# An overflow expert's tokens 65 to 96 computed before the branch for the tokens past 96

## The chip, the cores and the metric

The kernel runs on one core of one Trainium2 chip. The metric is the device time of one execution in microseconds (us). TensorE (PE; PEld is its weight load) does the matmuls, VectorE (DVE) and ScalarE (ACT) the elementwise work, and the queue of SyncE (SP) issues the loads of the weights.

## The reference, cut to what matters

256 tokens pass through a layer of attention and convolution, then a mixture of 32 experts, then a second block. The part that the change touches is the mixture:

```python
logits = (xt @ router_w + router_b).astype(jnp.float32)
top_vals, top_idx = lax.top_k(logits, 4)
top_w = jax.nn.softmax(top_vals, axis=-1)
combine = jnp.einsum('tk,tke->et', top_w, jax.nn.one_hot(top_idx, 32))
...
u = xt @ w1 + b1                     # w1 of an expert: 1024 x 2048
glu = jnp.minimum(u[:, ::2], 7.0)
lin = jnp.clip(u[:, 1::2], -7.0, 7.0)
a = glu * jax.nn.sigmoid(1.702 * glu) * (lin + 1)
out = a @ w2 + b2                    # w2 of an expert: 1024 x 1024
acc = acc + gate_e[:, None] * out
```

Each expert's weights are 12 MB in float32. An expert needs to compute only the tokens that chose it. With the inputs of this case the router sends 65 tokens to expert 5, 81 to expert 16, and at most 56 to any other; none gets more than 96.

## The kernel before

The weights of the whole program stream through a ring of SBUF slots in a fixed order: `w1` of an expert (8 slots of 1 MB), its `w2` (4 slots), `w1` of the next expert, and so on. All loads are issued by SP's queue, in order (lines 169, 175 and 190, in `pump`). A load into a used slot waits until the last reader of that slot is done. `ring.release` is called for the `w1` slots behind `over()` and for the `w2` slots behind the second matmul.

The loop over the 32 experts (from line 1213) gathers an expert's first 64 tokens by a one-hot matmul, multiplies by `w1` (`w1_mm`, line 1076), applies the gated activation on DVE and ACT (`glu`, lines 1088 to 1092), multiplies by `w2` (`w2_mm`, lines 1100 to 1108, or `w2_mm32`, lines 1114 to 1121, with up to 32 tokens) and scatters the result into the accumulators Y (`scatter`, line 1135). Between `glu` and the scatter of the expert before stands `over()`: under a branch on the count (line 1237) the code for tokens past 64. There `wide` handles 64 tokens from 96 on, under its own branch (line 1171), and calls itself for 160 and 224; `narrow` handles tokens 65 to 96: one-hot on DVE (`pmc` line 1030, `S_x` line 1034), gather (line 1040), scatter matrix (lines 1055 to 1059), `w1_mm`, `glu`, `w2_mm32`, scatter with `GT_x`. Both read the expert's `w1` and `w2` slots again, and both use the buffers S_x, GT_x, M2 and misc0.

Two facts of the program's text matter below. Each matmul adds one to a counter of PE; where a branch skips a body, a block on the other side (the else block) waits for what precedes it on PE and then adds the body's whole number at once, so that the count behind the branch is the same either way. And a load into a slot waits for the count of the last instruction, in the order of the program, that reads the slot.

A prefetch hint for PE at the start of an expert (`over_hint`, line 1164) names the branch of line 1237 and, in a register, which way it will go; DVE and ACT have none.

## Time and profile before

| | us |
|---|---|
| time, median of 3 runs | 1654.56 (1653.56 to 1656.74) |
| the profiled execution, time | 1654.44 |
| the profiled execution, span of its instructions | 1652.6 |
| PE busy | 1440.6 (87%) |
| DVE busy | 577.4 (35%) |
| ACT busy | 408.5 (25%) |
| weights read, at what mean rate | 531.60 MB, 322 GB/s |

The span runs from the first to the last instruction; 1.8 us of the execution lie outside it. The experts run from about 203 to 1157 us. In a row of the page with 40 slices a slice is 41.3 us. In rows of work, `128x32` and the like are partitions by elements; `[5.65 <-DVE S_x L1034]` is the idle time of the engine just before, and what ended it. A name with q (PEldq, SPq) is the engine's sequencer: it branches, waits or issues.

### The profile page before, as it was taken

Reading aid. Unit: us, or ns where it says so; the run is one execution under the profiler, and the core shown is the slowest. Engines: PE = TensorE matmul, PEld = TensorE weight load, DVE = VectorE, ACT = ScalarE, POOL = GpSimd, SP = SyncE. Lnnn points to the kernel's source line nnn. Section 1 sums busy time; section 2 is a strip of 40 time slices with the busy share of each in tenths; the row PEclk is TensorE's granted clock in tenths of the full one; section 3 lists DMA queues with packets and bytes.
Section 4 is the critical chain, followed back from the end, with each engine's and each line's share of the span. In section 5 each row is a group of like instructions: output and inputs, shape, how many; then the busy total and the mean of one; then the engine's idle time right before and its main releaser. Section 6 shows DMA issues by size and latency. Waiting matters only on the chain. (4 is left out here: it accounts for less than half of the span.)

```text
span 1652.6 us, 22025 instructions
## 1 busy us (share of the span) xinstructions
PE 1440.6 (87%) x9176; PEld 874.2 (53%) x9176; DVE 577.4 (35%) x1028; ACT 408.5 (25%) x664; POOL 19.8 (1%) x23
## 2 busy tenths in 40 slices
PE   5999988888987787687988898776999999999998
PEld 2877733343322332333333332321867999899997
DVE  2466602112210211111111111111896556565655
ACT  3455301001100001001000110001536344463434
POOL 0000200000000000000000000000000001000000
PEclk9999998979989879888998999888999999999999
DMA  9767899988999999999999999999915535245420
GB/s 392 289 258 300 318 399 398 423 360 344 423 422 420 423 421 420 422 377 386 424 419 389 424 420 421 423 422 419 363 49 205 212 147 223 109 180 228 167 88 26
DMA packets 66825, 535.27 MB, mean 324 GB/s; under 512 B 6992, under 2 KB 7504, under 8 KB 17104
## 3 DMA queue, kind: packets, MB, share of 16 engines
q1 hardware_dynamic: 65744, 531.36, 78.3%
q8 instruction: 132, 2.16, 0.5%
q10 hardware_dynamic: 896, 1.31, 0.2%
q14 instruction: 53, 0.43, 0.1%
HBM read 531.60 MB, written 1.05 MB: 322 GB/s over the span
## 5 line engine op out<-in xcount | busy, mean ns | idle before, releaser
L1076 PE MATMUL U<-ra,M 128*32 128x512 f32 (+1 forms) x1248 | 205.2, 631 | 42.1 <-DMA ra<-in_w_dram 36.1
L378 PE MATMUL G<-hTh,whl 128*128 128x256 f32 x720 | 201.2, 279 | 1.0 <-DVE whl L361 1.0
L376 PE MATMUL G<-hTh,whl 128*128 128x256 f32 x720 | 201.2, 279 | 0.1
L377 PE MATMUL G<-hTl,whl 128*128 128x256 f32 x720 | 200.9, 279 | 0.0
L361 DVE TENSOR_TENSOR whl<-ra,whl 128x1024 fp32r<-128x1024 f32 x160 | 185.9, 1221 | 21.0 <-ACT whl L358 20.9
L358 ACT ACTIVATE whl<-ra 128x1024 fp32r<-128x1024 f32 x159 | 156.7, 1046 | 7.5 <-ACT whl L358 4.8
L1088 DVE TENSOR_SCALAR M<-U 128x256 f32<-128x256 f32 (+1 forms) x34 | 17.9, 527 | 363.4 <-PE U L1076 363.4
L1076 PEld LDWEIGHTS U<-ra,M 128*32 128x32 f32 (+1 forms) x1248 | 51.6, 122 | 170.7 <-issue 121.1
L378 PEld LDWEIGHTS G<-hTh,whl 128*128 128x128 f32 x720 | 135.5, 188 | 1.4 <-DVE whl L361 1.4
L376 PEld LDWEIGHTS G<-hTh,whl 128*128 128x128 f32 x720 | 135.5, 188 | 1.1 <-ACT whl L358 0.3
L377 PEld LDWEIGHTS G<-hTl,whl 128*128 128x128 f32 x720 | 135.5, 188 | 0.7
L1089 ACT ACTIVATE M<-M 128x256 f32<-128x256 f32 (+1 forms) x34 | 17.0, 499 | 429.0 <-DVE M L1088 429.0
L1126 DVE SCALAR_TENSOR_TENSOR M<-misc,gc,g2hc 128x512 f32<-128x512 f32 x32 | 24.0, 751 | 230.2 <-PE misc L1108 123.9
L1135 PE MATMUL Y<-OO,GT 64*128 64x512 f32 x256 | 44.5, 468 | 54.6 <-PEq L1237 52.8
L1076 PE MATMUL U<-rc,M 128*64 128x512 f32 (+1 forms) x400 | 74.8, 634 | 11.3 <-DMA rc<-in_w_dram 11.3
L1050 ACT ACTIVATE M<-misc 128x512 f32<-128x512 f32 x32 | 19.1, 597 | 262.7 <-PE misc L1049 262.7
L1076 PE MATMUL U<-wa,M 128*32 128x512 f32 (+1 forms) x416 | 76.8, 622 | 0.1
L1049 PEld LDWEIGHTS misc<-S,h 128*128 128x128 f32 x512 | 59.6, 192 | 25.6 <-issue 25.6
L1135 PEld LDWEIGHTS Y<-OO,GT 64*128 64x128 f32 x256 | 27.7, 211 | 84.3 <-issue 79.3
L376 PE MATMUL Y<-whl,gh 128*128 128x512 f32 x176 | 69.5, 395 | 0.0
L376 PE MATMUL Y<-hTh,whl 128*128 128x256 f32 x224 | 66.3, 296 | 3.7 <-ACT whl L358 3.0
L377 PE MATMUL Y<-whl,gh 128*128 128x512 f32 x176 | 69.4, 394 | 0.0
(408 smaller groups left out, 2061.7 us busy)
## 6 DMA issues: line engine op xcount, KB each, us to landing
ra<-in_w_dram SPq DMA_DIRECT2D x64, 2048.0 KB, 24.7
ra<-in_w_dram SPq DMA_DIRECT2D x94, 1024.0 KB, 19.3
wa<-in_w_dram SPq DMA_DIRECT2D x71, 1024.0 KB, 22.9
rc<-in_w_dram SPq DMA_DIRECT2D x21, 2048.0 KB, 25.3
rc<-in_w_dram SPq DMA_DIRECT2D x30, 1024.0 KB, 24.1
ra<-in_w_ada_dram SPq DMA_DIRECT2D x24, 1024.0 KB, 11.9
ra<-in_w_up_dram SPq DMA_DIRECT2D x21, 1024.0 KB, 6.0
ra<-in_w_down_dram SPq DMA_DIRECT2D x21, 1024.0 KB, 7.0
```

What stands on the lines that cost most here:

```text
L358: act.activation(self.t[j][:, 0, :], src, AF.Copy)
L361: dve.tensor_tensor(self.t[j][:, 1, :], self.w[:, 1024 * j:1024 * (j + 1)], self.t[j][:, 0, :].bitcast(F32), ALU.subtract)
L376: pe.matmul(ps, lh, rh, start=start, stop=False)
L377: pe.matmul(ps, lh, rl, start=False, stop=False)
L378: pe.matmul(ps, ll, rh, start=False, stop=stop)
L1049: pe.matmul(ps[:, k], h2[:, t, kk * P:(kk + 1) * P], Sp[:, :, t, 0:C], start=(t == 0), stop=(t == 1))
L1050: act.activation(xg[:, 4 * q:4 * q + 4], ps, AF.Copy)
L1076: pe.matmul(U[o:o + n, j // m, :], xg(k), w1s[k][:, 512 * j:512 * (j + 1)], start=(k == 0), stop=(k == KT - 1), tile_position=(0, o))
L1088: dve.tensor_scalar(g, uv[:, :, :, 0], 7.0, None, ALU.min)
L1089: act.activation(s_, g, AF.Sigmoid, scale=1.702)
L1126: dve.scalar_tensor_tensor(t32, o_ps, gc, g2hc, ALU.mult, ALU.mult)
L1135: pe.matmul(y[t][h], GT[hs, t * P:(t + 1) * P], o[hs, :], start=False, stop=stop and o is ol)
```

## The change

`over()` calls `narrow` first and `wide` behind it, so that the branch of line 1171 on the count past 96 stands behind the work on tokens 65 to 96. The outermost branch of `wide` gets a label in `over()`, and a hint for it on PE, DVE and ACT is placed first in the body of `over()`.

```diff
     def wide(base, cv, e, S_x, sel, w1s, w2s, oh, ol):
-        with tc.If(cv > base):
+        with tc.If(cv > base, label=f"rest{e}" if base == C + 32 else None):
...
         def over():
             with tc.If(cv_e > C, label=f"over{e}"):
+                tc.mark_branch_hint_location(f"rest{e}", hint=cv_e > C + 32, engines=[ET.PE, ET.DVE, ET.Activation])
+                narrow(e, S_x, sel, w1s, w2s, Oh[b], Ol[b])
                 wide(C + 32, cv_e, e, S_x, sel, w1s, w2s, Oh[b], Ol[b])
-                narrow(e, S_x, sel, w1s, w2s, Oh[b], Ol[b])
```

From here on line numbers are those of before up to 1237; behind it the new program's are one higher.

On PE, at the start of an overflow body (here expert 5's; rc, wa and ra are slots of the ring), before:

```order
L1237 COMPARE_AND_BRANCH
L1171 COMPARE_AND_BRANCH
L1040 MATMUL misc_1737<-S_x,h_1543 128x64 x16
L1055 MATMUL misc_1737<-comb,S_x 128x1 x2
L1057 MATMUL misc_1737<-cst,S_x 128x128 x2
L1076 MATMUL U<-rc_3990,M_1714 64x512 x4
```

and now:

```order
L1237 COMPARE_AND_BRANCH
L1238 REGISTER_ALU
L1744 BRANCH_PREFETCH_HINT
L1040 MATMUL misc_1737<-S_x,h_1543 128x32 x16
L1055 MATMUL misc_1737<-comb,S_x 128x1 x2
L1057 MATMUL misc_1737<-cst,S_x 128x128 x2
L1076 MATMUL U<-rc_4026,M_1714 32x512 x4
```

The 32-wide gather has moved up to the branch of line 1237, and the branch of line 1171 is gone from ahead of it.

On PE, at the end of expert 5's `narrow`, before:

```order
L1135 MATMUL Y_110<-OO,GT_x 128x512
L1135 MATMUL Y_109<-OO,GT_x 128x512
L1135 MATMUL Y_110<-OO,GT_x 128x512
L1237 UNCONDITIONAL_BRANCH x2
L1067 TENSOR_LOAD cnt
L1135 MATMUL Y_107<-OO,GT_1730 128x512
```

and now:

```order
L1135 MATMUL Y_110<-OO,GT_x 128x512
L1135 MATMUL Y_109<-OO,GT_x 128x512
L1135 MATMUL Y_110<-OO,GT_x 128x512
L1171 COMPARE_AND_BRANCH
L1040 MATMUL misc_1737<-S_x,h_1543 128x64 x16
L1055 MATMUL misc_1737<-comb,S_x 128x1 x2
L1057 MATMUL misc_1737<-cst,S_x 128x128 x2
L1076 MATMUL U<-rc_4026,M_1714 64x512 x4
```

Behind the scatter of `narrow` now stand the branch of line 1171 and the three bodies of `wide`, whose matmuls on the `w1` slots (the last row, for one slot) are the last in the program to read them. SP's loads stand in the same order as before.

## Rows read from the trace of the kernel before

**Rows 1.** The page, 40 slices of the span: share of the weight-load engines, rate

```profile
DMA  9767899988999999999999999999915535245420
GB/s 392 289 258 300 318 399 398 423 360 344 423 422 420 423 421 420 422 377 386 424 419 389 424 420 421 423 422 419 363 49 205 212 147 223 109 180 228 167 88 26
```

**Rows 2.** Stretches: length, busy time by engine, granted clock, DMA share, GB/s

```profile
364.00:374.00 10.00, 9.48 (x58) 4.24 (x61) 0.16 (x1) 0.77 (x2) 0.00 (x0) 0.63 0.36 132
402.00:410.00 8.00, 7.08 (x63) 2.30 (x56) 2.72 (x9) 0.42 (x1) 0.00 (x0) 1.00 0.20 51
706.00:708.00 2.00, 2.00 (x24) 0.60 (x20) 0.00 (x0) 0.00 (x0) 0.00 (x0) 1.00 0.82 311
729.00:733.00 4.00, 4.00 (x22) 1.36 (x20) 0.00 (x0) 0.00 (x0) 0.00 (x0) 1.00 0.84 324
740.00:748.00 8.00, 7.18 (x64) 2.36 (x57) 1.80 (x5) 0.42 (x1) 0.00 (x0) 1.00 0.30 107
895.00:901.00 6.00, 2.16 (x14) 1.42 (x13) 2.87 (x5) 0.63 (x1) 0.00 (x0) 0.95 0.52 191
```

**Rows 3.** Timeline of SP's queue: start, length, line, load, count

```profile
371.22 0.33 SPq L190 DMA_DIRECT2D wa<-in_w_dram  x1
...
407.71 0.33 SPq L190 DMA_DIRECT2D rb<-in_w_dram  x1
...
706.32 0.33 SPq L190 DMA_DIRECT2D wa<-in_w_dram  x1
...
745.79 2.02 SPq L190 DMA_DIRECT2D ra<-in_w_dram  x4
...
898.79 2.57 SPq L190 DMA_DIRECT2D ra<-in_w_dram  x4
```

**Rows 4.** Waits of SP's queue, 355 to 415 us: total, times, longest

```profile
SPq L190 <- PE U L1076: 26.5, 2, 26.0
...
SPq L190 <- PEq L1237: 11.5, 1, 11.5
```

**Rows 5.** Line 1171, by stretch around each overflow: count, shortest/median/longest ns, start

```profile
L1171 PEldq COMPARE_BRANCH  x1: 7517/7517/7517, 350.4 to 350.4; - x1
...
L1171 PEldq EVENT_SEMAPHORE  x1: 51/51/51, 358.0 to 358.0; - x1
...
L1171 PEldq COMPARE_BRANCH  x1: 7295/7295/7295, 686.0 to 686.0; - x1
```

**Rows 6.** Timeline of PE and DVE around the two overflow starts

```profile
350.92 1.94 PE L1076 MATMUL U<-ra,M 128*64 128x512 f32 x8
...
355.86 0.17 DVE L1030 TENSOR_SCALAR pmc<-posm 128x2 f32<-128x2 f32 x1
358.07 0.48 DVE L1034 TENSOR_SCALAR S_x<-cst,pmc 128x128 f32<-128x128 f32 x2 [2.04 <-PEq L1171]
...
358.51 7.01 PE L1040 MATMUL misc<-S_x,h 128*128 128x32 f32 x32 [5.65 <-DVE S_x L1034]
...
693.40 0.48 DVE L1034 TENSOR_SCALAR S_x<-cst,pmc 128x128 f32<-128x128 f32 x2 [1.84 <-PEq L1171]
```

**Rows 7.** Timeline of PE at the end of each `narrow`

```profile
386.43 0.96 PE L1135 MATMUL Y<-OO,GT_x 64*128 64x512 f32 x6 [0.23 <-DVE OO L1128]
...
723.05 1.65 PE L1135 MATMUL Y<-OO,GT_x 64*128 64x512 f32 x6 [0.23 <-DVE OO L1128]
```

**Rows 8.** Line 1237 and its hint on PE, whole span: count, shortest/median/longest ns

```profile
L1237 PEldq COMPARE_BRANCH  x34: 78/444/6930, 206.0 to 1145.1; - x34
...
L1743 PEldq BRANCH_PREFETCH_HINT  x32: 30/35/44, 202.7 to 1123.3; - x32
```

**Rows 9.** PE behind a skipped line 1237, by two experts; and last wait for weights

```profile
302.26 1.20 PE L1135 MATMUL Y<-OO,GT 64*128 64x512 f32 x8 [0.57 <-PEq L1237]
...
865.18 1.20 PE L1135 MATMUL Y<-OO,GT 64*128 64x512 f32 x8 [4.00 <-PEq L1237]
...
1143.25 1.94 PE L1076 MATMUL U<-rc,M 128*32 128x512 f32 x8 [3.28 <-DMA rc<-in_w_dram]
```

**Rows 10.** Stretches of PE at half clock (columns as in rows 2)

```profile
357.70:371.40 13.70, 12.37 (x58) 9.04 (x62) 0.64 (x3) 0.77 (x2) 0.00 (x0) 0.50 0.62 261
692.20:705.90 13.70, 11.54 (x54) 8.84 (x58) 0.64 (x3) 0.77 (x2) 0.00 (x0) 0.50 1.00 419
866.30:873.10 6.80, 6.05 (x22) 3.18 (x22) 0.16 (x1) 0.98 (x2) 0.00 (x0) 0.50 0.99 405
```

## Prediction

> **What bounds the kernel now.** The page's slices come first. From slice 10 on (413 us) the rate stands at 420 to 424 GB/s almost throughout the experts; the exceptions are slices 8 and 9 (330 to 413 us, 360 and 344), 17 and 18 (702 to 785 us, 377 and 386) and 21 (868 to 909 us, 389) [rows 1]. So the experts run at the speed of the weight loads, and what costs time there is a stretch in which no load is under way. The last expert still waits 3.28 us for its weights at 1143 us [rows 9], so a load that comes later ends the expert stage later by as much.

> Next, where the load engines starve [rows 2]. Behind expert 5's first matmuls: 364 to 374 us at a share of 0.36, and 402 to 410 us at 0.20. Behind expert 16's: 706 to 708 at 0.82, 729 to 733 at 0.84, 740 to 748 at 0.30. And 895 to 901 at 0.52. These are the slices with the low rate, and two of the three groups are the two experts that enter the overflow code.

> Then what ends each gap. SP's next loads start at 371.22 and 407.71, and at 706.32, 745.79 and 898.79 [rows 3]. The one at 371.22 had waited 26.0 us for a `w1` matmul of PE (L1076), the one at 407.71 had waited 11.5 us for the sequencer at L1237 [rows 4]. This contrast is the row to look at. At 407.71 the expert is an ordinary one: its `w1` matmuls were done, but the last reader of its slots in the program is the skipped overflow body, so the load waits for the else block of L1237, which adds the skipped count. At 371.22 `narrow` had been entered and was itself the last reader, so slots came free matmul by matmul, in the middle of its `w1`.

> Last, the branch that moves. On PE, the branch at L1171 takes 7.5 us at expert 5 and 7.3 at expert 16 [rows 5]: a jump over the unused code. DVE has `pmc` at 355.86 and then sits 2.04 us (1.84 at expert 16) until that branch lets it write S_x; PE sits 5.65 us in all [rows 6].

> **The change part by part.** The profile gives each term; all of them happen twice, at experts 5 and 16. Where a branch is not entered nothing is added to the instructions that run.

> *The front of the overflow.* The branch leaves the head, so S_x follows `pmc` at once: 2.04 us earlier at expert 5, 1.84 at expert 16 [rows 6], and all of `narrow` with it. The hint costs PE some 35 ns [rows 8], and its register instruction, as an estimate, the same; DVE and ACT run theirs while PE is late anyway, so I count nothing, and with that cover gone 0.1 us.

> *The clock.* Both gathers run at half the granted clock (0.50 for 13.7 us [rows 10]), behind 5.65 us of idle PE. The idle shrinks to some 3.6 us. [...] An idle of 4.00 us elsewhere was followed by 0.50 [rows 9, 10], which is the nearest row, so I take 0, with 5.4 as the other end.

> *The back of the overflow.* Behind `narrow`'s scatter PE meets L1171 and jumps. With an effective hint the price is that of a skipped L1237: 0.57 us of idle PE [rows 9]. Without, that branch took 7.5 [rows 5]; with the matmuls still in flight some 6 of these remain. Of the hinted branches of L1237 the shortest took 78 ns, the median 444 and the longest 6930 [rows 8]; most are short, and here the hint comes some 35 us ahead (350.4 [rows 5] to about 385), so I take 0.6. In the loads' account PE's 0.6 is hidden, since the loads wait for the else block and not for what PE does behind it.

> [...]

> *The release of the slots: the term that decides.* Now the three bodies of `wide` stand last in the program and read `w1`. So at experts 5 and 16 the refill no longer waits for `narrow`'s own `w1` matmuls but for the else block of L1171, behind `narrow`'s last matmul; this is the ordinary expert's case of 11.5 us [rows 4], with the whole of `narrow` in between. SP's queue is in order, so every later load is queued behind that one, and the loads issued before had all landed when the gap began.

> Expert 5: `narrow`'s last matmul ends at 386.43 + 0.96 = 387.39 [rows 7]; less 2.04 it is 385.35. The refill moves from 371.22 [rows 3] to there: **+14.1 us** of empty queue. Against it stands the second gap. From 385.4 the queue has the 8 slots of `w1` and soon the 4 of `w2`, 12 loads of 1.05 MB, 29.8 us at 422 GB/s, to about 416; the next expert frees its slots at 407.71 less about 1.4. So the gap of 402 to 410, 8 x 0.80 = **6.4 us**, goes. Net **+7.7**.

> Expert 16: the last matmul ends at 723.05 + 1.65 = 724.70 [rows 7], less 1.84 = 722.86; the refill moves there from 706.32: **+16.5**. Here the queue was just running out at 706 (0.82 in that stretch), so up to 1.5 us of it may still be covered. The gaps of 729 to 733 (4 x 0.16 = 0.6) and 740 to 748 (8 x 0.70 = 5.6) go, since the refill lasts 29.8 us to 753 and the next release comes at 745.79. Net **+10.3**.

> Slice 21: the gap of 895 to 901 (6 x 0.48 = **2.9**) arises since PE lags the loads. They are 10 us later against PE than before, so the release at 898.79 comes in time. **-2.9**.

> Do PE's own inputs suffer? Expert 6's `w1` is in SBUF when the queue runs dry, its `w2` is the first thing refilled, four loads or 10 us, done by 397 and needed behind 408. So PE does not wait within the gap, and the delay shows as later weights only.

> Sum against the profiled execution: 1654.44 + 7.7 + 10.3 - 2.9 = **1669.5 us**; it lies 0.1 under the median of the runs, so this is the predicted median too.

> **The rivals.**

> 1. *Faster: the release doesn't move.* If a slot of an overflow expert were still freed by `narrow`'s matmuls, or if the loads had enough other slots, only front and back would count: -2.04 - 1.84 + 2 x 0.6 = -2.7, about 1652, and 1642 with the clock's 5.4 twice. It decides on whether the first load behind the gap follows `narrow`'s `w1` or its end. Against it: the wait of 11.5 us at L1237 shows that a skipped last reader holds the slots. Such a time is within 0.2% (3.3 us, about what a measurement of this kernel can tell from no change) of the time before, or a little better. 5%.

> 2. *The hint at L1171 does not work.* The branch then ends some 6 us behind the last matmul, and the else block with it: +6 at each expert, 1675.5 for one, 1681.5 for both. For: the slowest branches of L1237 had a hint as well (6930 ns). 13%, mostly for one.

> 3. *The clock stays up.* Both `narrow` end up to 5.4 us earlier: 1669.5 - 10.8 = 1659 at the least, 1664 with one of the two. 12%.

> 4. *The gap at 895 us stays*, since PE comes to wait for the later weights and releases late again: 1672.4. 8%.

> **How the numbers follow.** The forecast as summed, within some 3 us for the tail of the queue at 706 us and the run-to-run scatter, has 62%. The range must reach rival 4, one clock of rival 3 and one failed hint: **1663 to 1677**, which leaves out both hints failing, both clocks staying, and rival 1. Slower by over 0.2%: 0.94; within: 0.04; faster: 0.02, the last two both from rival 1.

> **What would show it.** In the trace of the changed kernel: SP's first load in the gap behind expert 5 starts some 14 us later against the gap's begin and names the sequencer at L1171, not a matmul of L1076; one long gap of about 20 us in the loads stands at each of the two experts, and the second gap, some 37 us behind the first before, is gone; the rate of slice 21 is back near 420. The front is right if S_x follows `pmc` without idle time; the back, if PE's branch at L1171 takes under 1 us. The forecast is wrong if the loads behind expert 5 restart in the middle of `narrow`, or if the changed program keeps its two gaps as they were.

## The result and the profile after

The changed kernel takes **1671.3 us** (median of 4 runs, 1669.39 to 1672.64), the kernel before beside it 1655.65 (4 runs, 1653.56 to 1657.09): a ratio of **1.010, 95% interval 1.008 to 1.0119**, 15.6 us slower. The forecast was 1669.5 with a range of 1663 to 1677. The profiled execution took 1669.99 us, 15.55 more than that of before; its span is 1668.2.

The page first, the same two rows of the 40 slices as in [rows 1]; a slice is 41.7 us here:

```profile
DMA  9767899977999999969999999999805544345420
GB/s 393 295 250 310 319 404 385 422 330 292 418 423 421 423 421 421 423 287 420 421 422 421 422 422 420 424 422 419 349 24 205 218 175 194 134 177 224 162 95 26
```

Slices 8 and 9 (334 to 417 us) have fallen from 360 and 344 GB/s to 330 and 292 and slice 17 (709 to 751) from 377 to 287, while slice 18 has risen from 386 to 420 and slice 21 from 389 to 421. So the loads stand still longer at exactly the two experts with an overflow, and once instead of twice.

What SP's queue waited for, the waits of 355 to 415 us and of 690 to 760 us (total, times, longest), against [rows 4]:

```profile
SPq L190 <- PEq L1171: 40.3, 1, 40.3
SPq L190 <- PEq L1237: 11.5, 1, 11.5
...
SPq L190 <- PEq L1171: 33.2, 1, 33.2
```

In the place where a `w1` matmul (L1076) released SP after 26.0 us, PE's sequencer at L1171 now does, after 40.3. The ordinary expert's 11.5 us at L1237 is as it was. The timeline of SP's queue, the rows that answer to [rows 3]:

```profile
386.22 0.33 SPq L190 DMA_DIRECT2D wa<-in_w_dram  x1
...
412.01 0.33 SPq L190 DMA_DIRECT2D rb<-in_w_dram  x1
...
730.11 0.33 SPq L190 DMA_DIRECT2D wa<-in_w_dram  x1
...
754.80 1.75 SPq L190 DMA_DIRECT2D ra<-in_w_dram  x4
```

How empty the load engines are in between (columns as in rows 2; the last two are the share of the load engines and GB/s):

```profile
364.00:366.00 2.00, 1.50 (x10) 1.17 (x10) 0.00 (x0) 0.39 (x1) 0.00 (x0) 0.50 0.96 401
366.00:386.00 20.00, 15.81 (x115) 4.20 (x114) 3.41 (x8) 1.81 (x4) 0.00 (x0) 0.89 0.02 7
402.00:410.00 8.00, 8.00 (x76) 3.40 (x78) 2.89 (x8) 1.11 (x2) 0.00 (x0) 1.00 0.99 420
...
706.00:714.00 8.00, 7.50 (x46) 2.73 (x50) 0.16 (x1) 0.77 (x2) 0.00 (x0) 0.65 1.01 423
714.00:721.00 7.00, 4.66 (x42) 1.14 (x38) 1.61 (x4) 0.80 (x2) 0.00 (x0) 1.00 0.58 246
721.00:730.00 9.00, 7.15 (x40) 1.98 (x32) 1.64 (x3) 0.63 (x1) 0.00 (x0) 0.74 0.01 4
740.00:748.00 8.00, 8.00 (x54) 3.67 (x54) 1.05 (x2) 1.11 (x2) 0.00 (x0) 1.00 1.03 430
```

At expert 5 the loads stand for 20 us in one piece, and the second gap of [rows 2] (402 to 410 us at 0.20) is full at 0.99. At expert 16 the queue is not dry at once: it runs at 0.58 for 7 us and stands for 9. Both pieces matter below.

The front and the back of `narrow`, from the timelines of DVE and PE at expert 5 with PE's branches at L1171 (345 to 400 us), then of PE at expert 16, against [rows 6] and [rows 7]:

```profile
357.82 0.16 DVE L1030 TENSOR_SCALAR pmc<-posm 128x2 f32<-128x2 f32 x1
358.02 0.48 DVE L1034 TENSOR_SCALAR S_x<-cst,pmc 128x128 f32<-128x128 f32 x2
...
358.45 5.52 PE L1040 MATMUL misc<-S_x,h 128*128 128x32 f32 x32 [3.40 <-DVE S_x L1034]
...
L1171 PEldq COMPARE_BRANCH  x2: 196/274/353, 385.2 to 386.3; - x2
...
385.14 0.95 PE L1135 MATMUL Y<-OO,GT_x 64*128 64x512 f32 x6 [0.23 <-DVEq L1171]
386.96 1.73 PE L1135 MATMUL Y<-OO,GT 64*128 64x512 f32 x8 [0.87 <-PEq L1171]
...
728.50 1.48 PE L1135 MATMUL Y<-OO,GT_x 64*128 64x512 f32 x6 [0.23 <-DVEq L1171]
730.85 2.07 PE L1135 MATMUL Y<-OO,GT 64*128 64x512 f32 x8 [0.86 <-PEq L1171]
```

S_x follows `pmc` with no idle between them, PE waits 3.40 us instead of 5.65, and behind the last scatter the jump over the three bodies costs PE 0.87 us of idle; the branch itself takes 353 ns, from 385.2 us on. What the change set out to save is saved; the release of the slots takes more than all of it.

To size each stretch I use one more number, worked out from the records of the load queue's packets: the **delay of the loads**, the moment at which the queue has moved a given number of bytes, less the moment at which it had moved as many in the profiled run of before. It grows where loads stand still for longer, or run more slowly, than before. The columns are its growth over a stretch, named by the times of before: at expert 5 (340 to 440 us), at expert 16 (680 to 800), at slice 21 (860 to 940), and its level at 1130 us, near the last expert.

| run | expert 5 | expert 16 | slice 21 | level at 1130 |
|---|---|---|---|---|
| after | +8.7 | +5.6 | -3.2 | +11.4 |
| the same kernel again (e8) | +8.6 | +5.0 | -3.1 | +11.3 |
| e1, slots freed by `narrow` | +3.4 | -2.5 | -2.8 | -2.1 |
| e2, half of them freed | +2.4 | -4.9 | -2.6 | -3.3 |
| e3, old order, slots held | +8.9 | +7.4 | -3.1 | +12.3 |
| e4, no hint at L1171 | +10.4 | +8.0 | -2.8 | +14.5 |
| e5, only expert 5 held | +6.9 | -0.9 | -1.3 | +4.1 |
| e6, only expert 16 held | +3.1 | +7.2 | -3.3 | +7.8 |
| e7, the program of before | +1.3 | +0.6 | -2.5 | +0.6 |

The last line is the yardstick: another run of the same instructions as before differs in single stretches by 0.6 to 2.5 us.

### The profile page after: what moved, and what is told of

The parts are those of the page before. It is cut to its first block, busy times and chain, and to the rows that moved or that the text cites. A ratio compares the mean times of both kernels' runs of the same rounds, so it can differ in the third digit from the quotient of the medians.

```text
span 1668.2 us, 22034 instructions
## 1 busy us (share of the span) xinstructions
PE 1457.5 (87%) x9176; PEld 877.1 (53%) x9176; DVE 577.5 (35%) x1028; ACT 408.9 (25%) x664; POOL 19.8 (1%) x23
## 3 DMA queue, kind: packets, MB, share of 16 engines
HBM read 531.60 MB, written 1.05 MB: 319 GB/s over the span
## 5 line engine op out<-in xcount | busy, mean ns | idle before, releaser
L1076 PE MATMUL U<-ra,M 128*32 128x512 f32 (+1 forms) x1248 | 208.6, 635 | 43.0 <-DMA ra<-in_w_dram 37.6
L1076 PEld LDWEIGHTS U<-ra,M 128*32 128x32 f32 (+1 forms) x1248 | 51.9, 123 | 173.6 <-issue 119.7
L1076 PE MATMUL U<-rc,M 128*64 128x512 f32 (+1 forms) x400 | 75.7, 644 | 13.1 <-DMA rc<-in_w_dram 13.1
L1076 PE MATMUL U<-wa,M 128*32 128x512 f32 (+1 forms) x416 | 77.9, 626 | 0.6 <-DMA wa<-in_w_dram 0.5
L1108 PE MATMUL misc<-ra,aT_t 128*64 128x512 f32 x264 | 68.6, 676 | 2.2 <-ACT aT_t L1101 2.2
L376 PE MATMUL Y<-whl,gh 128*128 128x512 f32 x176 | 69.5, 395 | 0.0
```

Of the source, the lines that this page charges most:

```text
L376: pe.matmul(ps, lh, rh, start=start, stop=False)
L1076: pe.matmul(U[o:o + n, j // m, :], xg(k), w1s[k][:, 512 * j:512 * (j + 1)], start=(k == 0), stop=(k == KT - 1), tile_position=(0, o))
L1108: pe.matmul(o_ps[C * h:C * h + C, :], lhs, w2s[n][:, hb, 512 * h:512 * (h + 1)], start=(kk == 0), stop=(kk == KT - 1), tile_position=(0, C ...
```

## The experiments

Theory: the time went up since the skipped bodies of `wide` became the last readers of `w1` in the program, so that the else block of L1171, behind all of `narrow`, frees the slots. Rivals: the work itself in its new order costs the time (the jump behind `narrow`, the clock); or it is the hint.

**e1: the order of the change, the slots freed early.** The unused bodies of `wide` read `w2` slots where they read `w1`; nothing that runs is changed.

```diff
-            w1_mm(sel, w1s, lambda k: xg_x[:, C * k:C * (k + 1)])
+            w1_mm(sel, [w.rearrange("p a b -> p (a b)") for w in w2s for _ in range(2)], lambda k: xg_x[:, C * k:C * (k + 1)])
```

> The changed kernel, except that wide's first product reads the expert's w2 slots in place of its w1 slots; that body is for tokens past 96, of which these inputs have none, so the instructions that run are the same. The w1 slots' last reader is then narrow itself. Theory (the moved release costs the time): SP's refill behind expert 5 follows narrow's w1 matmuls again, the two gaps of the loads are back as before, and only front and back count: 1655.7 - 4 + 2 x 0.9, about 1652 to 1654. Rival (the order of the work, the branch behind narrow or the hint cost the time): 1671, as the changed kernel.

Measured: 1655.97 us (12 runs) beside 1657.53 for before (26), ratio 0.9991 (0.997 to 1.0012). SP's wait of 355 to 420 us and its first loads in the two gaps:

```profile
SPq L190 <- PE U L1076: 23.2, 2, 22.7
...
368.06 0.33 SPq L190 DMA_DIRECT2D wa<-in_w_dram  x1
...
706.63 0.33 SPq L190 DMA_DIRECT2D wa<-in_w_dram  x1
```

The releaser is a matmul of L1076 again, and the whole loss is gone with the order and the hint still in place. That fells the rival by which the order itself makes the loss of time. The gain that I expected beyond that isn't there to be seen: the interval holds no change.

Nor are the two gaps back "as before". Behind `narrow` PE's granted clock falls for a while (0.58 in 387 to 397 us, where before has 1.00), and the load that waits for the second product of the ordinary tokens (L1108) is let go later. Before, then e1, one stretch of all engines (columns as in rows 2) and SP's wait in 376 to 420 us:

```profile
387.00:397.00 10.00, 9.25 (x54) 4.17 (x50) 0.16 (x1) 0.98 (x2) 0.00 (x0) 1.00 1.01 424
...
SPq L175 <- PE misc L1108: 13.8, 1, 13.8
```

```profile
387.00:397.00 10.00, 9.07 (x34) 4.74 (x36) 0.16 (x1) 0.98 (x2) 0.00 (x0) 0.58 0.52 206
...
SPq L175 <- PE misc L1108: 20.5, 1, 20.5
```

So with early slots a gap opens here that neither the kernel before (share 1.01) nor the changed one has, whose refill is still under way (0.92). e6, whose slots at expert 5 are free as well, has it too (394 to 396 us at 0.07). The delay at expert 5 grows by 3.4 us in e1 and 3.1 in e6, where e7 has 1.3. At expert 16 e1 gains 2.5, and its time shows neither.

**e2: half of the slots freed.** As e1, but the bodies keep reading the last four `w1` slots.

```diff
-            w1_mm(sel, w1s, lambda k: xg_x[:, C * k:C * (k + 1)])
+            w2v = [w.rearrange("p a b -> p (a b)") for w in w2s]
+            w1_mm(sel, w2v + w1s[4:], lambda k: xg_x[:, C * k:C * (k + 1)])
```

> The changed kernel, except that wide's first product reads w2 slots for its first four pieces and w1 slots for the last four (not run with these inputs). Half of the w1 slots are then freed by narrow's matmuls, the other half by the else block of L1171. Theory (what counts is the time the loads stand still, and a later second gap is given back): 4 to 5 MB refill from about 371 to 382 us, a gap of some 4 us until 386, none at 402; about 10 us of standstill at expert 5 against 12.7 before, so 1650 to 1657. Rival (each slot held costs its share): half-way between the changed kernel and the one above, about 1662.

Measured: 1657.06 us (10 runs), ratio 1.0005 (0.9987 to 1.0023), at the edge of the theory's bounds and off the rival's 1662. SP starts again with the freed slots and then meets the held ones (timeline and waits, 355 to 420 us, and the stretch behind the freed ones, columns as in rows 2):

```profile
369.81 0.33 SPq L190 DMA_DIRECT2D wa<-in_w_dram  x1
...
SPq L169 <- PEq L1171: 14.0, 1, 14.0
...
381.00:388.00 7.00, 4.35 (x35) 2.02 (x24) 1.64 (x3) 0.63 (x1) 0.00 (x0) 0.94 0.21 52
```

The four loads ahead of it cover the wait of 14.0 us on L1171 until about 381 us; in 381 to 388 us the load engines are nearly empty. The details came out otherwise than expected: this gap is 5.5 us long (7 x 0.79) where some 4 were forecast, and the one that was to be gone is there, 408 to 413 us at a share of 0.13. At expert 5 the loads lose 2.4 us all the same and at expert 16 they gain 4.9, so in the time half of the slots can't be told from all of them.

**e3: the order of before, the slots held.** `over()` is as before, and eight one-column matmuls behind `narrow` read the `w1` slots.

```diff
                 wide(C + 32, cv_e, e, S_x, sel, w1s, w2s, Oh[b], Ol[b])
                 narrow(e, S_x, sel, w1s, w2s, Oh[b], Ol[b])
+                for w in w1s:
+                    pe.matmul(bank0[0:1, 0:1], w[:, 0:1], ident[:, 0:1], start=True, stop=True)
```

> The kernel before, its order and branches untouched, with eight matmuls of one column behind narrow's scatter, each reading one of the w1 slots into a bank that is free, so that narrow's end frees the slots. Theory: the refill behind experts 5 and 16 starts at narrow's end, some 16 and 18 us later than before (no gain at the front), so 1655.7 + 15.6 + about 2 to 3: 1671 to 1677. Rival (the new order or the branch behind narrow costs the time): 1656 to 1657.

Measured: 1670.29 us (7 runs), ratio 1.0062 (1.0041 to 1.0083); the profiled run took 1670.86. SP's wait, its two late starts, and PE's branch at L1171 at expert 5 (345 to 395 us):

```profile
SPq L190 <- PE misc L1241: 41.7, 1, 41.7
...
386.13 0.33 SPq L190 DMA_DIRECT2D wa<-in_w_dram  x1
...
731.08 0.33 SPq L190 DMA_DIRECT2D wa<-in_w_dram  x1
...
L1171 PEldq COMPARE_BRANCH  x1: 7386/7386/7386, 347.0 to 347.0; - x1
```

The branch still stands at the front and takes 7.4 us, no code was moved, and most of the loss is there: the late release alone makes most of it. The size is a miss. Against the 1655.7 that they were worked out from, the 1671 to 1677 expected are 1.0092 to 1.0129, above the whole interval, and single runs lie between 1660.93 and 1672.97. The interval just overlaps that of the change (1.008 to 1.0119) and well that of e8 (1.0055 to 1.0102).

**e4: the change without its hint.**

```diff
             with tc.If(cv_e > C, label=f"over{e}"):
-                tc.mark_branch_hint_location(f"rest{e}", hint=cv_e > C + 32, engines=[ET.PE, ET.DVE, ET.Activation])
                 narrow(e, S_x, sel, w1s, w2s, Oh[b], Ol[b])
```

> The changed kernel without the line that marks the hint. Theory: PE's branch at L1171 behind narrow takes 6 to 7.5 us instead of 0.35, the else block and the refill behind it come some 6 us later at each of the two experts, with no second gap left to give it back: 1671.3 + 12 = 1683 (1679 to 1687). Rival (the hint does nothing, the branch is short since narrow's code lies ahead of it): 1671.

Measured: 1669.47 us (4 runs), ratio 1.0079 (1.0064 to 1.0093): a miss. PE's branches at L1171 in 380 to 390 us (the long one is the jump), `narrow`'s last scatter, and SP's first load:

```profile
L1171 PEldq COMPARE_BRANCH  x2: 187/1734/3281, 384.0 to 387.5; - x2
...
384.00 1.50 PE L1135 MATMUL Y<-OO,GT_x 64*128 64x512 f32 x6 [0.23 <-DVEq L1171]
...
387.44 0.33 SPq L190 DMA_DIRECT2D wa<-in_w_dram  x1
```

The jump takes 3.3 us here (3.7 at expert 16), not 7.5, and begins while the scatter's matmuls still run. Those end at 384.00 + 1.50 = 385.50, so the load starts 1.9 us behind them; at expert 16 it is 2.9 (729.17 + 0.97 = 730.14 to 732.99). Neither the theory's 6 to 7.5 us nor the rival's short jump came.

**e5 and e6: one expert held at a time.** In e6 the 5 is a 16.

```diff
-            w1_mm(sel, w1s, lambda k: xg_x[:, C * k:C * (k + 1)])
+            w2v = [w.rearrange("p a b -> p (a b)") for w in w2s for _ in range(2)]
+            w1_mm(sel, w1s if e == 5 else w2v, lambda k: xg_x[:, C * k:C * (k + 1)])
```

> The changed kernel, but the unused wide bodies read w1 only at expert 5; at every other expert they read w2 slots in its place (wrong numbers, had they run; they are skipped), so that only expert 5's w1 slots are held until the else block of L1171. Theory (two holds that add up): expert 5's stall is that of the changed kernel (21.9 us of standing loads in 345 to 430 us, against 15.7 with both released), expert 16's that of the released version (4.7). Standing loads of the experts then 31.4 + 6.2 = 37.6 us against 33.4 before: about 4 us slower than before, 1658 to 1662. Rival (one hold alone makes PE late enough to pay for all, the second is nearly free): +10 or more, 1666 to 1671.

> The same with the roles changed: the unused wide bodies read w1 only at expert 16, and w2 slots everywhere else (wrong numbers, had they run). Theory (two holds that add up): expert 16's stall is that of the changed kernel (13.6 us in 690 to 780 us, against 4.7 released), expert 5's that of the released version (15.7): 31.4 + 8.9 = 40.3 us against 33.4 before, about 7 us slower than before, 1660 to 1665; with the run before it the two excesses over the released version make the whole 15 us of the change. Rival (the second hold is nearly free once the first has been paid): +10 or more, 1666 to 1671.

Measured beside 1656.47 for before (24 runs): only expert 5 held, 1659.24 us (10 runs), ratio 1.0022 (1.0005 to 1.0039); only expert 16 held, 1662.11 (5 runs), ratio 1.0044 (1.0028 to 1.0061). SP's first loads in the two gaps, of e5 and then of e6:

```profile
384.27 0.33 SPq L190 DMA_DIRECT2D wa<-in_w_dram  x1
...
708.83 0.33 SPq L190 DMA_DIRECT2D wa<-in_w_dram  x1
```

```profile
369.29 0.33 SPq L190 DMA_DIRECT2D wa<-in_w_dram  x1
...
726.61 0.33 SPq L190 DMA_DIRECT2D wa<-in_w_dram  x1
```

As far as the intervals can tell, each about 0.17% to either side, the two holds add up, each at its place. Counted from the released version (0.9991, of another session) they are 0.31% and 0.53%, together 0.84%; from there the changed kernel stands at 0.88% in the same session as these (e8).

**e7: the order of before, with a second hint ahead.** The hint for L1171 stands beside that for L1237 at the start of the expert, to save the 7.4 us at the front without moving the release.

```diff
         tc.mark_branch_hint_location(f"over{e}", hint=cv > C, engines=[ET.PE])
+        tc.mark_branch_hint_location(f"rest{e}", hint=cv > C + 32, engines=[ET.PE])
...
-        with tc.If(cv > base):
+        with tc.If(cv > base, label=f"rest{e}" if base == C + 32 else None):
```

> The kernel before, its order untouched (wide first, then narrow, so narrow is the last reader of w1), with the label on the branch of L1171 and its hint on PE beside the hint of L1237 at the start of the expert. It takes the one thing the change gains (no 7.4 us jump at the front) without its loss. Theory (a hint that comes early makes a jump cheap wherever it stands): L1171 takes under 1 us at experts 5 and 16, S_x follows pmc, narrow and the release in it come some 2 us earlier at each: 1650 to 1654. Rival (two hints at one place don't both hold, or the jump costs its 7 us anyway since its target was not kept): L1171 still takes over 3 us, 1654 to 1658; if the hint of L1237 is lost by it, some 0.5 to 5 us more at each expert in PE, partly hidden, and slower than 1658.

Measured: 1654.91 us (12 runs), ratio 0.9996 (0.9983 to 1.0009). The hints and the branch of L1171 on PE, whole span (lines are one higher, so it is L1172):

```profile
L1744 PEldq BRANCH_PREFETCH_HINT  x32: 30/35/44, 203.0 to 1124.7; - x32
...
L1172 PEldq COMPARE_BRANCH  x2: 7157/7218/7280, 353.1 to 688.5; - x2
```

There are 32 hints as in [rows 8]: the second one left no instruction, and the program is that of before, instruction for instruction. So the experiment says nothing on a hint placed early; whether one would help there stays open. It serves as a second profile of the kernel before, which turns out to matter.

**e8: the changed kernel again**, unaltered, beside e5 to e7.

> The changed kernel unaltered, beside the others on one chip, as their yardstick and to stand against the run without the hint (1.0079 of before). Theory (the hint is worth 1 to 2 us of release at each expert): ratio to before 1.004 to 1.007 if the two sessions were alike, but the first one gave 1.010; so within 0.3% of 1.0079 it says that the hint cannot be told from none in the time: 1664 to 1673.

Measured: 1669.52 us (4 runs), ratio 1.0079 (1.0055 to 1.0102), against 1.010 (1.008 to 1.0119) in the first session. PE's last scatter at expert 5 ends at 385.90 + 1.45 = 387.35 and the load follows at once:

```profile
385.90 1.45 PE L1135 MATMUL Y<-OO,GT_x 64*128 64x512 f32 x6 [0.22 <-DVEq L1171]
...
387.48 0.33 SPq L190 DMA_DIRECT2D wa<-in_w_dram  x1
```

Its ratio equals that of e4, so the hint can't be told from none in the time, though the traces give it 1.8 us at expert 5 (1.9 against 0.13) and 2.7 at expert 16, and the delay at 1130 us is 3.2 lower (11.3 for 14.5). What lies behind the experts scatters by as much: from the first matmul of the second block to the end of the span it is 494.0 us in e8 and 490.1 in e4, 493.4 in before and 490.8 in e7.

## Why the prediction was right, and where it was not

The mechanism and the total were right. Some terms were off, in both directions, and the total is better than its parts.

**The release: right.** The line to watch was SP's first load behind expert 5, and who lets it go. It names L1171, as forecast. Counted from PE's branch at L1237, at the start of the overflow, it came at 371.22 - 350.3 = 20.9 us before [rows 3] and comes at 386.22 - 352.4 = 33.8 now: +12.9, for a forecast of +14.1. At expert 16 it was 706.32 - 685.8 = 20.5 and is 730.11 - 694.3 = 35.8: +15.3 for +16.5. PE's branches at L1237 in before and after, first at expert 5 (340 to 400 us), then at expert 16 (680 to 745); the overflow's own is the first of each row:

```profile
L1237 PEldq COMPARE_BRANCH  x2: 78/128/179, 350.3 to 386.4; - x2
...
L1237 PEldq COMPARE_BRANCH  x1: 78/78/78, 352.4 to 352.4; - x1
...
L1237 PEldq COMPARE_BRANCH  x3: 78/195/622, 685.8 to 743.6; - x3
...
L1237 PEldq COMPARE_BRANCH  x1: 78/78/78, 694.3 to 694.3; - x1
```

Both are a little smaller, since `narrow` is a little faster than forecast. e1 and e3 take the release apart from the order: without it the loss is gone, and by itself it makes most of it.

**Expert 5: right.** +8.7 for +7.7: the delay of the loads rises by 15.4 until 385 us and falls by 6.7 up to 440, where 14.1 and 6.4 were counted. (The 15.4 are more than the 12.9 since PE came to this overflow 2.1 us later than before; over the ten profiles its branch at L1237 lies anywhere from 346.8 to 352.9 us.) The second gap went as described, with a load stream that is full at 0.99 in 402 to 410 us. Both this and the next size are taken against one profile of before; against e1, which holds no slots, the change loses 5.3 us at expert 5 and 8.1 at expert 16.

**Expert 16: mis-sized.** +5.6 (5.0 in e8) for +10.3. The failed step is the queue "just running out at 706", of which I thought up to 1.5 us to be covered, from a share of 0.82 over 2 us, and took none off the sum. The rows of after show the tail that was left: a share of 0.58 for 7 us, so 4.1 us of loads, before 9 us of standstill. Together 2.9 + 9 = 11.9 us of standstill in place of the 16.5 counted; the second gap gave back 7 where 6.2 was counted. What the queue still held at 706 us could not be read from its share there, since in the old trace the next load came just then.

**Slice 21: right in the sum, wrong in its reason.** -3.2 for -2.9. But e7, which is the program of before, and e1, which holds nothing, have the gain as well. The stretch of 780 to 930 us in before, then in e7 (last column GB/s):

```profile
780.00:930.00 150.00, 130.50 (x668) 51.85 (x661) 24.28 (x51) 12.44 (x23) 0.00 (x0) 0.92 0.99 413
```

```profile
780.00:930.00 150.00, 130.38 (x682) 51.62 (x674) 24.27 (x51) 12.45 (x23) 0.00 (x0) 0.92 1.01 420
```

So the gap at 895 us belonged to that one profiled run of before, not to the kernel: in all nine other profiles the delay falls there, by 1.3 to 3.3 us. A delay of the loads by 10 us was not needed to close it, and that the term came out is luck. Rival 4, by which the gap would stay, speaks of nothing that the kernel has to have.

**What the sum lacked.** The delay at the last expert is 11.4 us, yet the profiled run is 15.55 longer. Of the 11.4, about 0.9 arose ahead of expert 5 (the delay goes from -0.5 to +0.4 in 205 to 290 us), where the change does nothing. The rest comes behind the loads. The last wait for weights [rows 9] and the first matmul of the second block, in after; in before the latter was at 1159.17:

```profile
1156.81 1.93 PE L1076 MATMUL U<-rc,M 128*32 128x512 f32 x8 [3.76 <-DMA rc<-in_w_dram]
...
1174.26 3.67 PE L1342 MATMUL G<-cst,x_b 128*128 128x128 f32 x16 [0.79 <-DVE x_b L1313]
```

The wait ends 1156.81 - 1143.25 = 13.6 us later, so the last weights land 2.2 us later than the bytes' delay says; the time from there to the second block is 17.45 us instead of 15.92, with the last group of L1076 at 1.88 us where before had 1.06 (the granted clock is 0.50 in 1156 to 1162 us); and 0.5 comes after, within the scatter of the second block that e8 shows. Six of the eight other runs show 1.6 to 2.3 us of that late landing as well (e1 to e4, e6 and e8), with slots held or freed; e5 shows none and e7 0.9. So it isn't the release that makes it; why the weights land later than their bytes' delay was not found.

So 15.1 were predicted as 7.7 + 10.3 - 2.9, and 15.55 came as 8.7 + 5.6 - 3.2 + 0.9 - 0.6 (the start and the remaining stretches) + 2.2 + 1.5 + 0.5. That the two agree to half a microsecond is chance. What rests on the mechanism is the sum of the first two terms, 14.3 for 18.0 (13.4 counted from e1), and e3, e5 and e6 bear that out.

**The front: right, a little more.** The idle of PE shrank by 2.25 us (forecast 2.04), and the gather took 5.52 us instead of 7.01 [rows 6].

**The back: right for the jump.** PE's idle was 0.87 us for 0.6 and is hidden from the loads. That PE would then run at half clock (0.50 in 387.4 to 397.6 us) was not foreseen; the refill covers it here (share 0.95), and e1 shows what it takes where nothing covers it (share 0.52 in 387 to 397 us). Without the hint the branch took 3.3 and 3.7 us at this place (e4), with it 0.35.

**The rivals.** The failed hint (6 us each) didn't occur, and its price was mis-sized: the failed step is "with the matmuls still in flight some 6 of these remain". e4 shows 1.8 and 2.7 us, since the jump at this place takes half as long as at the front (3.3 and 3.7 us for 7.5 and 7.3). Rival 1, the release that doesn't move, is what e1 builds: its 1652 came out as 0.9991 of before, no gain that can be seen, and it leaves out the half clock behind `narrow` (0.58 in e1), which costs the loads at expert 5. (With the clock's 5.4 twice its sum gives 1641, not 1642.) The clock's 5.4 us at each expert, in rivals 1 and 3 and behind the range, is an estimate: half of the gather's 7.01 us [rows 6] and of the 3.9 from 367.5 us to the end of the half clock [rows 10]. No run shows it; what came is small, with a gather of 5.52 us at expert 5 and 5.88 at expert 16 where before had 7.01 and 7.00. Two stretches of after, columns as in rows 2, against [rows 10]:

```profile
360.10:370.30 10.20, 9.68 (x49) 5.93 (x52) 0.16 (x1) 0.77 (x2) 0.00 (x0) 0.50 0.61 259
...
387.40:397.60 10.20, 9.45 (x32) 4.24 (x30) 0.16 (x1) 0.98 (x2) 0.00 (x0) 0.50 0.95 373
```

The half clock begins 1.6 us behind the start of the gather and lasts 10.2 us instead of 13.7, so the start of the gather ran at a granted clock of 1.00 (358.0 to 360.1 us). A new stretch at 0.50 follows behind the jump, 387.4 to 397.6 us. The loads run through it at a share of 0.95, so the changed kernel doesn't pay for it in loads. The jump is not shown to be its cause: in 387 to 397 us the clock is 0.50 to 0.61 in all profiles but before and e7 (1.00 in both), also in e3, which has no jump there.

## What to carry to other kernels

Where loads into used slots wait for the last reader in the order of the program, code that never runs is a reader as well: put behind code that runs, it holds the slots until the branch around it has been passed (SP's waits of 40.3 and 33.2 us on L1171). Before a rare block is moved, look at what its skipped reads hold and which queue stands behind that; here two savings of some 2 us cost two stalls, and the old order, rare code first, is the better one. None of the versions tried beats the kernel before by more than the measurement can tell (e1: 0.9991, 0.997 to 1.0012).
